# Moving the reload of gated outputs and the tail's loads in the last head of a recurrent mixer

## The chip, the cores and the metric

The kernel runs on one core of one Trainium2 chip. The metric is device time in microseconds (us) of one execution. The engines are TensorE (PE; PEld is its weight load), VectorE (DVE), ScalarE (ACT), GpSimd (POOL) and SyncE (SP). Each executes its own queue of instructions in order; SP, ACT and POOL also issue DMA transfers, each on a queue of its own, and all transfers run on the core's 16 DMA engines.

## The reference, cut to what matters

One step of a two-layer trunk over 640 tokens (512 latent, 128 context) of width 1024. Layer 0 is a gated grouped-query attention. Layer 1, in which the change lies, is a bidirectional gated linear recurrence (HGRN2) with 8 heads of 128 keys and 128 values:

```python
proj = h @ w_in                      # q, f_fw, f_bw, i_in, g: five blocks of 1024 columns
qh = silu(heads(q)); vh = heads(i_in)
forget = lb + (1 - lb) * sigmoid(f)  # for each direction
k = (1 - lb) * sigmoid(-f)
S = exp(b_last) * S + einsum(k * exp(b_last - b), v)     # scan, forward and backward
o = scores @ v + (q * exp(b)) @ S
o = rms_norm(o_fw + flip(o_bw), norm_gain)
gated = (o * silu(g)).astype(h.dtype)
out = gated @ w_out
x = layer_norm(ALPHA * x + gate * out, ln_gain, ln_bias)
```

Outputs are the new latent and context tokens, the attention's keys and values of the context, and the final states of the recurrence (`new_s`).

## The kernel before

All matrix products are done in a split form: an operand is written as a rounded high part and the remaining low part (`hi`, `lo`), and three products (hi·hi, hi·lo, lo·hi) are accumulated. A cast on ACT makes the high part, a subtraction on DVE or POOL the low part.

**Layer 1 runs head by head.** For each of the 8 heads `proj_gen` makes the five projections of the head on TensorE, and `gla_gen` then makes its recurrence. The two are generators that stop at `yield`; the main loop runs the projections of head h and, through a `Lane` with estimated times, lets the recurrence of head h − 1 advance between them. The projections of the last head (h = 7) have 23 steps: two for each of five token tiles (n = 0 to 9, the products `vgps`, lines 1377 and 1381), four for the query (n = 10 to 13, `rps`, lines 1403 to 1405), four for each direction's forget gate (n = 14 to 21), and one that ends them. The weights come as 512 KB pieces into three raw buffers (`raw`, line 239, on SP's queue); a cast on ACT (line 260) and a subtraction on DVE (line 262) turn a piece into `hi` and `lo`, and free its buffer. `pump` asks for raw pieces up to two ahead of their use: all 40 pieces of `rec_w_in`, then the 8 of `rec_w_out`.

**The recurrence** (`gla_gen`) is a tree over levels 0 to 6 of token blocks. At each level a key copy on ACT (`kc`, line 1651), in some levels also a query copy (`At`, line 1656), prepares TensorE's score products (`lv`, lines 1677 and 1683), and two DVE multiplications (`A`, lines 1701 and 1706) apply the decay. The blocks near the diagonal are gathered in `near` (lines 1668 and 1728) and written into the score tile `At` by four copies on POOL (`spread`, line 1715); the far blocks go there by copies on ACT (`place`, line 1721). Then come key transposes (`kp`, line 1766) and their copy `kt` (line 1768), state products (`sp`, line 1772), the state update on DVE (`S`), the final states' copies `ns` (line 1782) and stores (`new_s`, line 1783), the output products (`op`), the root of the mean square on POOL (`rstdo`, line 211), and the transposed, gated output (`oT`, line 1809). Heads 0 to 6 take their levels in pairs; the last head takes them one by one, with `spread` in level 4. The tile `ns` shares its buffer (tag `kc`) with the key copies.

**The gated outputs** of the first heads have no room in SBUF, since heads 1 to 6 use seven block products instead of eight and keep sums of the tokens (`thi`, `tlo`) in the buffers `hhi` and `hlo`. Those outputs are stored to DRAM (`gd`). With the last head the sums are done with, and `reload_gen` takes the two buffers as `ghi` and `glo`, loads the stored outputs into `glo` (line 1624, SP's queue, five loads of 320 KB), and makes for each a cast on ACT (line 1627) and a subtraction on DVE (line 1628). The three heads that end later write into `ghi` and `glo` directly (lines 1819 and 1820).

**The tail.** After the last projections the main program runs the end of head 6's recurrence, and then head 7's recurrence interleaved with the first output products (`outp`, lines 1211 to 1213) and the last pieces of `rec_w_out` (`tail_steps`). The epilogue of the output (class `Out`) multiplies with the gate (`y`, line 1257), adds the residual (line 1260) and normalises. It needs the gate rows (`gate[1]`, two loads of 512 KB, line 339) and the residual tiles `x1` (512 KB each, line 1913), all on POOL's queue. In the kernel before, the gate and the first two residual tiles are asked for before head 6's recurrence is finished.

**Order.** This half of the program is not run in the order in which it is written. A planner places each instruction on its engine's queue, by a model of time: of those that are ready, the one written first goes first, so a later-written instruction that is ready sooner overtakes. `tc.keep_in_program_order` ties an instruction behind all that was written before it on its engine, and `tc.issue_after(ins)` ties what is written in its block behind `ins` on that engine; neither adds a wait.

Of the kernel before, what the change touches and what calls it, by code (L numbers as in the profile page):

```python
# [11 lines left out]
F32 = mybir.dt.float32  # L12
# [6 lines left out]
P = 128  # L19
D = 1024  # L20
# [3 lines left out]
NT = TT * P  # L24
# [4 lines left out]
RH = 8  # L29
# [20 lines left out]
RES_AT = 6  # L50
SEVEN = range(1, RH - 1)
FORMS_AT = 3
D_GLA = 5.5
D_LEV = 2.7
D_PAIR = 6.0
# [12 lines left out]
def view(t, off, dims):  # L68
    base = t[:]
    return bass.AP(base.tensor, base.offset + off, [list(base.ap[0])] + [list(d) for d in dims])  # L70
# [76 lines left out]
def drain(gen):  # L147
    for _ in gen:
        pass
# [3 lines left out]
def hybrid_step(ctx: ExitStack, tc: tile.TileContext, a: dict, o: dict):  # L153
    nc = tc.nc
    PSUM = bass.MemoryType.PSUM

    def pool(name, bufs, **kw):
        return tc.tile_pool(name=name, bufs=bufs, **kw)
# [178 lines left out]
    def gate_load(layer, eng):  # L337
        for s in range(2):
            eng.dma_start(gate[layer][:, s, :], gated[layer][s:s + 1, :].to_broadcast((P, D)))
# [96 lines left out]
    gate = [None, None]  # L436
# [3 lines left out]
    def lpool(name, bufs):  # L440
        return left.enter_context(pool(name, bufs))
# [661 lines left out]
    side = Side()  # L1103
# [220 lines left out]
    KF, KB, QB, QF = 0, NT, 2 * NT, 3 * NT  # L1324
# [3 lines left out]

    last_gate = []
    outs_done = []  # L1330
    vg_done = []

    def held():
        st = ExitStack()
# [265 lines left out]
    def token_forms():  # L1600
        f11, f12, f22, f21 = sums
        for f, i, j in ((f11, 0, 0), (f12, 0, 1), (f22, 1, 1), (f21, 1, 0)):
            hi, lo = (t[:, 4 * i:4 * i + 4, slice(*HALVES[j])].bitcast(F32) for t in (h1hi, h1lo))
            with tc.issue_after(vg_done[0]):
                nc.vector.tensor_tensor(f, hi, lo, ALU.add)
            yield
        for dst, x, y in ((f11, f12, f11), (f12, f22, f12), (f22, f11, f22)):
            nc.vector.tensor_tensor(dst, x, y, ALU.subtract)
            yield
        nc.vector.tensor_tensor(f21, f21, f22, ALU.add)  # L1610
        yield
        for (hi, lo), f in zip(tokens, (f11, f22, f12, f21)):
            nc.scalar.copy(hi, f)
            yield
            nc.vector.tensor_tensor(lo, f, hi.bitcast(F32), ALU.subtract)
            yield

    def reload_gen():
        ghi = hp.tile([P, KT, NT], F32R, tag="hhi", name="ghi")
        glo = hp.tile([P, KT, NT], F32R, tag="hlo", name="glo")  # L1620
        gated_out.extend((ghi, glo))
        todo = list(spilled)
        for k in todo:
            nc.sync.dma_start(glo[:, k, :].bitcast(F32), gd[k])
        for k in todo:
            yield
            nc.scalar.copy(ghi[:, k, :], glo[:, k, :].bitcast(F32))
            nc.vector.tensor_tensor(glo[:, k, :], glo[:, k, :].bitcast(F32), ghi[:, k, :].bitcast(F32), ALU.subtract)

    cs = ExitStack()  # L1630
    g2 = cs.enter_context(pool("g2", 2, side="right"))
# [8 lines left out]
    def gla_gen(h, H):  # L1640
        A, T, v, g = H["A"], H["T"], H["vg"][:, :, 0, :], H["vg"][:, :, 1, :]
# [6 lines left out]
        def kcopy(w, tag="kc"):  # L1648
            nb = NT // (2 * w)
            kc = g1.tile([P, NT], F32, tag=tag, name="kc")  # L1650
            nc.scalar.copy(view(kc, 0, [[2 * w, nb], [w, 2], [1, w]]), view(A, KF, [[2 * w, nb], [KB - KF + w, 2], [1, w]]))  # L1651
            return kc

        def qcopy(w):
            nb = NT // (2 * w)
            nc.scalar.copy(view(At, 0, [[2 * w, nb], [w, 2], [1, w]]), view(A, QB, [[2 * w, nb], [QF - QB + w, 2], [1, w]]))
            return At

        kc = kcopy(1)
        yield D_GLA  # L1660
        near = g1.tile([P, 32 * TT], F32, tag="near", name="near")
        At = g1.tile([P, NT], F32, tag="At", name="At")

        def blocks(t, w):
            return t.rearrange("p (a b) -> p a b", b=w)
# [46 lines left out]
        def spread():  # L1712
            for b in range(4):
                r = slice(32 * b, 32 * b + 32)
                nc.gpsimd.tensor_copy(blocks(At[r, :], P)[:, :, r], blocks(near[r, :], 32))  # L1715

        def place(lev, pt):
            w = 1 << lev
# [11 lines left out]
        if pairs:  # L1730
            for lev in (1, 3, 5):
                if lev == 1:
                    yield D_TAIL
                    lane.finish(1)
                k2, _, _ = decay(lev, "on" if lev < 5 else None)
                yield D_FIRST if lev == 1 else D_PAIR if h < RH - 2 else 2 * D_LEV
                pt = wide(bank2("lv"))
                late = scores(pt[:, 512:], lev + 1, k2, None)
                with tc.issue_after(late):
                    scores(pt, lev, k1, q1)  # L1740
                k1, q1, last = decay(lev + 1, "kc" if lev < 5 else None, lev < 5)
                if lev < 5:
                    merge(lev, pt)
                    merge(lev + 1, pt[:, 512:])
                else:
                    spread()
                    place(5, pt)
                    place(6, pt[:, 512:])
        else:
            for lev in range(1, 7):  # L1750
                yield D_LEV
                pt = wide(bank2("lv"))
                scores(pt, lev, k1, None)
                k1, _, last = decay(lev, "kc" if lev < 4 else None)
                if lev < 5:
                    merge(lev, pt)
                else:
                    place(lev, pt)
                if lev == 4:
                    spread()  # L1760
# [56 lines left out]
        ghi, glo = gated_out  # L1817
# [51 lines left out]
    def wo_piece(n, after=()):  # L1869
        nh, i = OUT1[n]  # L1870
        hi, lo = slots[2 * n], slots[2 * n + 1]
        wo[nh, i] = tuple(t.rearrange("p (k n) -> p k n", k=2) for t in (hi, lo))
        split_piece(hi, lo, ("rec_w_out", nh, i), nc.vector, after)

    def wr_slots():
        w = wr.tile([P, 2, 1024], F32R, tag="w", name="rw")
        slots.extend(w[:, i, :] for i in range(2))
# [9 lines left out]
    side = token_forms()  # L1887
    for h in range(RH):
        H = {} if h else H
        if h == RH - 1:  # L1890
            sxs.close()
            side = reload_gen()
            next(side, None)
        for n, dt in enumerate(proj_gen(h, H, False) if h else first):
            lane.advance(dt)
            if h or n >= FORMS_AT:
                next(side, None)
            if h == 0 and n == RES_AT:
                residual.compute()
                residual.loads()  # L1900
        lane.add(gla_gen(h, H))
# [4 lines left out]
    ghi, glo = gated_out  # L1906
# [4 lines left out]
    def load_resid(tt, t):  # L1911
        resid[tt] = t
        tc.keep_in_program_order(nc.gpsimd.dma_start(t, x1a[tt]))

    def out_k(tt, k):
        if tt not in outs:
            outs[tt] = bank2("outp", "pj" if tt < 2 else "b2")
        for nh in range(2):
            out_mms(outs[tt], tt, nh, ghi, glo, [k])

    def tail_steps():
        wr_slots()
        wo_piece(3)
        for tt in range(2):
            out_k(tt, 1)
        yield
        w2 = gsp.tile([P, 5, 1024], F32R, tag="gs", name="w2")
        w3 = h1p.tile([P, 5, 1024], F32R, tag="h1lo", name="w3")
        slots.extend(t[:, i, :] for t in (w2, w3) for i in range(5))
        wo_piece(4)  # L1930
        out_k(0, 2)
        yield
        todo = [(tt, k) for k in range(2, KT - 1) for tt in range(2)][1:]
        for n in range(5):
            if n < 3:
                wo_piece(n + 5)
            for tt, k in todo[2 * n:2 * n + 2]:
                out_k(tt, k)
            yield
        for ks in ((0,), (1,), (2,), (3, 4, 5), (6,)):  # L1940
            for k in ks:
                out_k(2, k)
            yield

    while not lane.gens[0][2]:
        lane.step(lane.gens[0])
    gate[1] = g2.tile([P, 2, D], F32, tag="A", name="gate1")
    gate_load(1, nc.gpsimd)
    xp = lpool("xp", 1)
    load_resid(0, xp.tile([P, D], F32, name="x1"))  # L1950
    load_resid(1, g2.tile([P, 2 * NT], F32, tag="T", name="x1")[:, :D])
    for tt in range(2):
        out_k(tt, 0)
    lane.finish(1)
    steps = tail_steps()
    for _ in lane.gens[0][0]:
        next(steps, None)
    drain(steps)
    gx.close()
# [129 lines left out]
```

## Time and profile before

| | us |
|---|---|
| median of 3 runs | 825.15 |
| the three runs | 823.31, 829.16, 825.15 |
| the profiled execution | 824.67 |
| its span | 822.9 |
| mean granted TensorE clock | 0.994 |

The time of an execution is that of the whole program on the device; the span is the profile's, from its first to its last instruction. In a timeline a row gives the start in us from the span's start, the length in us, the engine, the line of the kernel, the operation, output and inputs, and their shapes; where the engine was idle before, the length of that pause and the instruction that ended it stand in brackets. `x5` merges five neighbours. SPq, ACTq and POOL's rows of DMA give the time of issue, not that of the transfer. Rows of issues give the KB of each transfer and the median us from its issue to its landing.

### The profile page before, as it was taken

Reading aid. Unit: us, or ns where it says so; the run is one execution under the profiler, and the core shown is the slowest. Engines: PE = TensorE matmul, PEld = TensorE weight load, DVE = VectorE, ACT = ScalarE, POOL = GpSimd, SP = SyncE. Lnnn points to the kernel's source line nnn. Section 1 sums busy time; section 2 is a strip of 40 time slices with the busy share of each in tenths; the row PEclk is TensorE's granted clock in tenths of the full one; section 3 lists DMA queues with packets and bytes.
Section 4 is the critical chain, followed back from the end, with each engine's and each line's share of the span. In section 5 each row is a group of like instructions: output and inputs, shape, how many; then the busy total and the mean of one; then the engine's idle time right before and its main releaser. Section 6 shows DMA issues by size and latency. Waiting matters only on the chain.

```text
span 822.9 us, 19277 instructions
## 1 busy us (share of the span) xinstructions
PE 793.2 (96%) x7953; PEld 701.2 (85%) x7953; DVE 597.8 (73%) x1083; ACT 447.8 (54%) x890; POOL 214.9 (26%) x261
## 2 busy tenths in 40 slices
PE   8999999999999989999999999999999999998994
PEld 6779999878888766888999999999989999896874
DVE  3667767686678885676898787778687866977376
ACT  2252545566566786132565766667474847754242
POOL 0124001353434943011500324122321304131021
PEclk9999999999999999999999999999999999999998
DMA  9944243334130150621432343324132425224041
GB/s 324 395 147 165 103 154 131 103 106 153 52 129 27 40 191 30 227 103 54 136 104 66 91 114 98 105 68 126 54 126 65 114 90 171 84 89 172 31 156 76
DMA packets 36630, 98.12 MB, mean 119 GB/s; under 512 B 5296, under 2 KB 12480, under 8 KB 36544
## 3 DMA queue, kind: packets, MB, share of 16 engines
q1 hardware_dynamic: 25872, 78.95, 28.7%
q0 software_dynamic: 4768, 14.18, 6.0%
q10 hardware_dynamic: 5904, 3.78, 1.5%
q8 instruction: 62, 1.02, 0.5%
q14 instruction: 24, 0.20, 0.1%
HBM read 86.06 MB, written 10.83 MB: 118 GB/s over the span
## 4 chain that ended last, share of the span: by engine, by line
PE 78%; DVE 8%; ACT 5%; DMA 4%; issue 2%; POOL 2%; SPq 0%; ACTq 0%; DVEq 0%; POOLq 0%
PE vgps L1381 7%; PE vgps L1377 4%; PE pot L948 4%; PE outp L1211 4%; PE rps L1449 3%; PE rps L1403 3%; PE outp L1213 3%; PE outp L1212 3%; PE rps L1405 3%; PE rps L1404 3%; PE pt L1034 3%; PE rps L1451 3%; PE rps L1450 3%; PE acc L566 3%; PE lv L1677 2%
## 5 line engine op out<-in xcount | busy, mean ns | idle before, releaser
L1027 POOL TENSOR_SCALAR p<-p,rc 128x640 f32<-128x640 f32 x64 | 57.1, 897 | 115.2 <-DVE rc L1026 98.0
L1715 POOL COPY At<-near 32x160 f32<-32x160 f32 x32 | 14.2, 443 | 195.9 <-PE lv L1683 176.0
L1021 ACT ACTIVATE p<-sc,nm 128x640 f32<-128x640 f32 x64 | 51.2, 802 | 25.3 <-DVE nm L1016 15.6
L1016 DVE TENSOR_REDUCE nm<-sc 128x1 f32<-128x640 f32 x64 | 51.7, 816 | 12.6 <-PE sc L922 12.5
L1403 PE MATMUL rps<-h1hi,rw 128*128 128x320 f32 x176 | 55.4, 315 | 0.0
L1404 PE MATMUL rps<-h1lo,rw 128*128 128x320 f32 x176 | 54.4, 309 | 0.0
L1405 PE MATMUL rps<-h1hi,rw 128*128 128x320 f32 x176 | 54.4, 309 | 0.0
L1034 PE MATMUL pt<-small,p 128*128 128x128 f32 x320 | 49.0, 277 | 3.0 <-DVE pts L926 1.2
L1381 PE MATMUL vgps<-rw,h1hi 128*128 128x512 f32 x180 | 48.4, 393 | 0.1
L1034 PEld LDWEIGHTS pt<-small,p 128*128 128x128 f32 x320 | 36.5, 140 | 12.0 <-issue 5.6
L1651 ACT COPY kc<-A 128x640 f32<-128x640 f32 x47 | 37.5, 798 | 13.5 <-DVE A L1701 7.5
L926 ACT COPY pts<-pt 128x512 f32<-128x512 f32 x64 | 36.1, 590 | 14.7 <-PE pt L1034 14.5
L921 PE MATMUL sc<-kk,X 128*128 128x320 f32 x128 | 42.4, 340 | 1.7 <-ACT p L1021 1.6
L1721 ACT COPY At<-lv 32x160 f32<-32x160 f32 (+1 forms) x48 | 15.9, 331 | 51.0 <-PE lv L1683 50.6
L948 PE MATMUL pot<-pts,vv 128*64 128x256 f32 x320 | 38.3, 384 | 2.1 <-DVE pts L926 2.0
L378 PE MATMUL gps<-hhi,whi 128*128 128x320 f32 x128 | 40.0, 312 | 0.1
L379 PE MATMUL gps<-hlo,whi 128*128 128x320 f32 x128 | 39.6, 309 | 0.0
L380 PE MATMUL gps<-hhi,wlo 128*128 128x320 f32 x128 | 39.5, 309 | 0.0
L1381 PEld LDWEIGHTS vgps<-rw,h1hi 128*128 128x128 f32 x180 | 33.0, 188 | 7.1 <-DVE vg L1397 0.5
L922 PE MATMUL sc<-klo,X 128*128 128x320 f32 x128 | 38.5, 310 | 0.0
L1381 PE MATMUL vgps<-wspare,h1hi 128*128 128x512 f32 x140 | 38.2, 394 | 0.0
L387 PE MATMUL qmm<-whi,hhi 128*128 128x256 f32 x120 | 35.0, 292 | 0.1
(347 smaller groups left out, 2624.5 us busy)
## 6 DMA issues: line engine op xcount, KB each, us to landing
raw<-in_rec_w_in SPq DMA_DIRECT2D x40, 512.0 KB, 3.8
raw<-in_ada_m SPq DMA_DIRECT2D x16, 512.0 KB, 8.3
raw<-in_attn_w_in SPq DMA_DIRECT2D x16, 512.0 KB, 4.6
raw<-in_ada_s SPq DMA_DIRECT2D x16, 512.0 KB, 3.7
adaraw<-in_ada_c SPq DMA_DIRECT2D x11, 512.0 KB, 5.4
raw<-in_attn_w_out SPq DMA_DIRECT2D x8, 512.0 KB, 3.9
raw<-in_rec_w_out SPq DMA_DIRECT2D x8, 512.0 KB, 4.5
raw<-in_ada_c SPq DMA_DIRECT2D x5, 512.0 KB, 4.4
```

The lines of the kernel that those rows point to most:

```text
L378: nc.tensor.matmul(ps[:, :320], w.hi(k)[:, c], hhi[:, k, t], start=(k == 0), stop=False)
L379: nc.tensor.matmul(ps[:, :320], w.hi(k)[:, c], hlo[:, k, t], start=False, stop=False)
L921: nc.tensor.matmul(out, X[:, h, t0:t0 + P], kk[:, c, k0:k1], start=True, stop=False)
L948: nc.tensor.matmul(pot[j * HD:(j + 1) * HD, :CW], vv[:, slot, c * HD:(c + 1) * HD], moving[j], start=first, stop=last)
L1016: nc.vector.tensor_reduce(nm[:, 0:1], sc[:, :, :320], AX.XY, ALU.max, negate=True)
L1021: return nc.scalar.activation(halves(p[:]), sc[:, :, :320], AF.Exp, bias=nm[:, 0:1], accum_out=su[:, 0:1])
L1027: nc.gpsimd.tensor_scalar(p, p, rs[:, 0:1], 1.0, ALU.mult, ALU.mult)
L1034: nc.tensor.transpose(pt[:, i * 256 + q * P:i * 256 + (q + 1) * P], ps[q][:, (k0 + i) * P:(k0 + i + 1) * P], ident)
L1381: nc.tensor.matmul(out, h1hi[:, k, t], wvg[i][:, k % 4].rearrange("p e n -> p (e n)"), start=(k == 0), stop=(k == KT - 1))
L1403: nc.tensor.matmul(ps[:, j, :320], hi[:, k, :], h1hi[:, k, t], start=(k == 0), stop=False)
L1404: nc.tensor.matmul(ps[:, j, :320], hi[:, k, :], h1lo[:, k, t], start=False, stop=False)
L1405: nc.tensor.matmul(ps[:, j, :320], lo[:, k, :], h1hi[:, k, t], start=False, stop=(k == KT - 1))
```

## The change

Two things are moved; no computation is added or left out.

1. `reload_gen` takes its two buffers when the last head starts, as before, but stops there. It goes on at step 6 of the last head's projections, where it writes the five loads, rests during steps 7 to 11, and writes one pair of cast and subtraction per step from step 12 on. Each cast is tied behind the key copy that was written last at that time. Before, the loads were written at the head's start, and the pairs at steps 0 to 4, with no tie.
2. The loads of the gate and of the first two residual tiles are no longer written before the end of head 6, but inside head 7's recurrence, after the step that writes `spread`, and tied behind the last of its four copies on POOL.

```diff
+RELOAD_AT = 6
+RELOAD_OFF = ((), range(7, 12))
...
         todo = list(spilled)
+        yield
         for k in todo:
             nc.sync.dma_start(glo[:, k, :].bitcast(F32), gd[k])
         for k in todo:
             yield
-            nc.scalar.copy(ghi[:, k, :], glo[:, k, :].bitcast(F32))
+            with tc.issue_after(last_kc[0]):
+                nc.scalar.copy(ghi[:, k, :], glo[:, k, :].bitcast(F32))
             nc.vector.tensor_tensor(glo[:, k, :], ...)
...
-            nc.scalar.copy(view(kc, ...), view(A, KF, ...))
+            last_kc[:] = [nc.scalar.copy(view(kc, ...), view(A, KF, ...)).ins]
...
-                nc.gpsimd.tensor_copy(blocks(At[r, :], P)[:, :, r], blocks(near[r, :], 32))
+                spread_done[:] = [nc.gpsimd.tensor_copy(blocks(At[r, :], P)[:, :, r], blocks(near[r, :], 32)).ins]
...
-            next(side, None)
+            next(side)
         for n, dt in enumerate(proj_gen(h, H, False) if h else first):
             lane.advance(dt)
-            if h or n >= FORMS_AT:
+            if n >= (FORMS_AT if h == 0 else RELOAD_AT if h == RH - 1 else 0) and n not in RELOAD_OFF[h == RH - 1]:
                 next(side, None)
...
+    def tail_loads():
+        with tc.issue_after(spread_done[0]):
+            gate[1] = g2.tile([P, 2, D], F32, tag="A", name="gate1")
+            gate_load(1, nc.gpsimd)
+            xp = lpool("xp", 1)
+            load_resid(0, xp.tile([P, D], F32, name="x1"))
+            load_resid(1, g2.tile([P, 2 * NT], F32, tag="T", name="x1")[:, :D])
...
     while not lane.gens[0][2]:
         lane.step(lane.gens[0])
-    gate[1] = g2.tile([P, 2, D], F32, tag="A", name="gate1")
-    gate_load(1, nc.gpsimd)
-    xp = lpool("xp", 1)
-    load_resid(0, xp.tile([P, D], F32, name="x1"))
-    load_resid(1, g2.tile([P, 2 * NT], F32, tag="T", name="x1")[:, :D])
...
     steps = tail_steps()
+    spread_done.clear()
     for _ in lane.gens[0][0]:
+        if spread_done:
+            tail_loads()
+            spread_done.clear()
         next(steps, None)
```

More of the change, by code (lines that the diff above doesn't have):

```diff
@@ L1330, in hybrid_step @@
     outs_done = []
-    vg_done = []
+    vg_done, spread_done, last_kc = [], [], []
     def held():
@@ L1650, in kcopy @@
             kc = g1.tile([P, NT], F32, tag=tag, name="kc")
-            nc.scalar.copy(view(kc, 0, [[2 * w, nb], [w, 2], [1, w]]), view(A, KF, [[2 * w, nb], [KB - KF + w, 2], [1, w]]))
+            last_kc[:] = [nc.scalar.copy(view(kc, 0, [[2 * w, nb], [w, 2], [1, w]]),
+                                         view(A, KF, [[2 * w, nb], [KB - KF + w, 2], [1, w]])).ins]
             return kc
```

## The prediction

> **What bounds the kernel now.** I read the page first.
>
> ```profile
> span 822.9 us, 19277 instructions
> ...
> PE 793.2 (96%) x7953; PEld 701.2 (85%) x7953; DVE 597.8 (73%) x1083; ACT 447.8 (54%) x890; POOL 214.9 (26%) x261
> ```
>
> TensorE is busy for 793.2 of 822.9 us. The change removes no matrix work, so all that it can win is TensorE's idle time, and only that part of the 29.7 us that lies where it moves something: from the start of the last head (about 687 us) to the end of that head's scores (about 765 us). The profiled execution took 824.67 us, 1.8 over its span; the median of the three runs shown is 825.15, 0.5 above it. I make the sum on the profiled execution and add that 0.5.
>
> Next I read busy time by stretches of time and, for what ended each idle piece, the timelines of single engines.
>
> ```profile
> 745.00:750.00 5.00, 4.15 (x133) 3.33 (x131) 4.41 (x8) 3.21 (x5) 0.00 (x0) 1.00 0.99 382
> 750.00:755.00 5.00, 3.17 (x90) 2.15 (x88) 3.07 (x6) 1.67 (x2) 0.00 (x0) 1.00 0.21 82
> 763.00:775.00 12.00, 11.83 (x118) 9.65 (x117) 4.82 (x13) 3.00 (x7) 1.26 (x4) 1.00 0.00 1
> ```
>
> The columns are stretch, length, busy PE, PEld, DVE, ACT, POOL, granted clock, DMA share, GB/s. From 745 to 755 TensorE is idle for 0.85 + 1.83 = 2.68 us; in its first half the DMA engines are full (0.99, 382 GB/s). From 763 to 775 they carry nothing. The clock is 1.00, so it plays no part.
>
> ```profile
> 698.19 0.63 PE L1677 MATMUL lv<-A,kc 128*32 128x32 f32 x40 [0.88 <-ACT kc L1651]
> ...
> 708.53 0.52 PE L1677 MATMUL lv<-A,kc 128*32 128x32 f32 x38 [0.78 <-DVE A L1706]
> ```
>
> These are the two other TensorE gaps in reach, in the reload's stretch: 0.88 us for a key copy on ACT, 0.78 us for a decay step on DVE. So 0.88 + 0.78 + 2.68 = 4.34 us, 0.5% of the run, is the most that the change can win.
>
> **Part 1, the reload of gated outputs.** It has five loads on SP's queue and five pairs of an ACT cast and a DVE subtraction.
>
> ```profile
> 662.46 24.49 SPq L239 DMA_DIRECT2D raw<-in_rec_w_in  x4
> 687.32 2.22 SPq L1624 DMA_DIRECT2D glo<-gd  x5
> 690.70 55.68 SPq L239 DMA_DIRECT2D raw<-in_rec_w_out  x8
> ```
>
> *The loads.* The program writes the reload before the last head's projections, so also before the last three of these rec_w_in loads, which the projections' weight steps call for; yet it stands behind all four in the queue. The order is the planner's, by when a load's buffer is free: glo takes the buffer of the token sums, in use until head 6's last products. Written six steps later, the loads still come before the first rec_w_out load, which is written at step 14. I therefore expect them at the same place in the queue, at about 687 us: cost nothing, gain nothing. Were they really later, this would win:
>
> ```profile
> out_new_s<-ns ACTq DMA_DIRECT2D x16, 64.0 KB, 1.8
> ...
> out_new_s<-ns ACTq DMA_DIRECT2D x2, 64.0 KB, 7.2
> ...
> 697.13 1.00 ACT L1651 COPY kc<-A 128x640 f32<-128x640 f32 x1 [2.91 <-DMA out_new_s<-ns]
> ```
>
> The state stores land in 1.8 us at the median of sixteen, but in 7.2 us beside the reload (the second row is from 684 to 700 us). Their source shares its buffer with the key copy, so ACT waits 2.91 us and TensorE the 0.88 above. With the reload gone from there the 0.88 goes; with it in place it stays. I take 0 and keep 0.88 for a rival.
>
> *The casts move for certain*, since each is tied behind the key copy written last when its step comes.
>
> ```profile
> L1627 ACT CAST ghi<-glo x5: 711/732/748, 692.9 to 705.2; 128x640 fp32r<-128x640 f32 x5
> L1628 DVE TENSOR_TENSOR glo<-glo,ghi x5: 817/819/828, 693.8 to 706.0; 128x640 fp32r<-128x640 f32 x5
> ...
> 703.19 0.83 DVE L1628 TENSOR_TENSOR glo<-glo,ghi 128x640 fp32r<-128x640 f32 x1 [0.62 <-ACT ghi L1627]
> 703.93 0.69 DVE L1397 TENSOR_TENSOR vg<-vgps,low 128x512 f32<-128x512 f32 x1
> ...
> 707.57 0.82 DVE L1706 TENSOR_TENSOR A<-A,Tb 128x640 f32<-128x640 f32 x1
> ```
>
> Five casts of 0.73 us (3.7 us of ACT) and five subtractions of 0.82 us (4.1 us of DVE) leave 693 to 707 us. Two of them stand in the chain to the 0.78 gap. The subtraction at 703.19 makes DVE wait 0.62 for its cast and ends 0.74 later, where the next row starts; the one at 706.0 takes 0.8 more ahead of the decay step at 707.57, on which TensorE waits. Taking 0.8 to 1.5 us out of a chain that is 0.78 late removes that gap: gain 0.8. Next late there is TensorE's own queue, which is full.
>
> *Where they go* must hold them:
>
> ```profile
> 712.82 0.73 ACT L1651 COPY kc<-A 128x640 f32<-128x640 f32 x1 [0.23 <-DVE A L1701]
> 714.68 1.05 ACT L260 CAST w<-raw 128x1024 fp32r<-128x1024 f32 x1 [1.13 <-DMA raw<-in_rec_w_out]
> ...
> 719.42 0.73 ACT L1651 COPY kc<-A 128x640 f32<-128x640 f32 x1
> ...
> 724.37 2.04 ACT L1721 COPY At<-lv 32x160 f32<-32x160 f32 x6 [3.59 <-PE lv L1683]
> ...
> 723.78 0.83 DVE L1701 TENSOR_TENSOR A<-A,T 128x640 f32<-128x640 f32 x1 [0.82 <-PE lv L1683]
> ...
> 727.17 1.18 DVE L1512 TENSOR_SCALAR T<-s,omlb,lbt 128x640 f32<-128x640 f32 x1 [1.72 <-ACT s L1501]
> ...
> 727.77 1.04 PE L1766 MATMUL kp<-small,A 128*128 128x128 f32 x8
> ```
>
> At step 12 the last key copy written is the one at 712.82, from step 13 on the one at 719.42. The first cast (0.73) fits ACT's 1.13 us wait before 714.68; the other four, 2.9 us, fit the 3.59 us wait before 724.37. On DVE the last four subtractions, at 0.74 each back to back, are 3.0 us against idle pieces of 0.82 and 1.72 us. If all came before the decay at 723.78, its pair would end 3.0 − 0.82 = 2.2 us later, at about 727.6 instead of 725.4 (727.17 less the wait of 1.72), just ahead of the transposes at 727.77 that read it. Bounds: 0, and 1 us should a wait slip past them. I take 0.2, near the first, since the subtractions have no reader before the output products:
>
> ```profile
> L1211 PE MATMUL outp<-wx,ghi x10: 389/389/499, 738.9 to 800.7; 128*128 128x512 f32 x10
> ```
>
> **Part 2, the tail's loads.** Four loads of 512 KB on POOL's queue (two gate rows, two residual tiles) leave the stretch where the last weights come in.
>
> ```profile
> 739.26 1.12 POOL L339 DMA_DIRECT2D gate<-gated  x2 [9.03 <-PE op L1789]
> ...
> gate<-gated POOLq DMA_DIRECT2D x2, 512.0 KB, 5.4
> raw<-in_rec_w_out SPq DMA_DIRECT2D x2, 512.0 KB, 6.8
> x<-x1a POOLq DMA_DIRECT2D x2, 512.0 KB, 7.8
> ...
> raw<-in_rec_w_out SPq DMA_DIRECT2D x8, 512.0 KB, 4.5
> ...
> 747.50 1.06 ACT L260 CAST w<-raw 128x1024 fp32r<-128x1024 f32 x1 [1.22 <-DMA raw<-in_rec_w_out]
> ...
> 752.78 1.04 ACT L260 CAST w<-raw 128x1024 fp32r<-128x1024 f32 x1 [3.35 <-DMA raw<-in_rec_w_out]
> ...
> 749.29 0.39 PE L1212 MATMUL outp<-rw,ghi 128*128 128x512 f32 x1 [0.85 <-issue]
> ...
> 754.50 0.56 PE L1677 MATMUL lv<-A,kc 128*32 128x32 f32 x40 [1.82 <-ACT kc L1651]
> ```
>
> Beside them two weight loads take 6.8 us where the median of all eight is 4.5. ACT waits in order for the second, 3.35 us, with the key copy queued behind the weight's cast; TensorE waits 1.82 us for that copy. Landing in 4.5 us instead of 6.8 it is there 2.3 us sooner, and the scores at 754.50 could start at 752.2. TensorE reaches them at 754.50 − 1.82 = 752.68 from its own queue. So the 1.82 goes. The other 0.85 us is a gap that the profile lays to no engine, in the stretch where DMA is full. If it is a slow fetch of instructions, it goes too, and the scores start at 752.2: gain 2.3. From below the gain is 0, if the load is slow for another reason. I take 2.0.
>
> [...] No run here shows what that gap is.
>
> *The price.* The loads start behind the spread, with the last products' epilogue as their first reader:
>
> ```profile
> 763.21 1.39 POOL L1715 COPY At<-near 32x160 f32<-32x160 f32 x4 [18.91 <-DVE near L1668]
> ...
> 786.66 1.29 DVE L1257 TENSOR_TENSOR y<-outp,gate 128x512 f32<-128x512 f32 x2
> ```
>
> Issued from 764.6 (763.21 + 1.39), at 1.12 us of POOL for two, the last is out by 766.8 and lands by 774.6 even in 7.8 us, 12 us before 786.66, in a stretch with no other transfers. POOL itself is free there: the spread waited 18.91 us for its input. Queued behind the loads is only the last head's square root, whose input comes from TensorE's last product of that head. Cost 0; without that cover it would be the lateness itself, beyond 12 us.
>
> **Sum:** −0.8 + 0.2 − 2.0 = −2.6; 824.67 − 2.6 = 822.1 for a profiled execution, about 822.5 as a median (825.15 − 2.6).
>
> **Rivals.** *The reload really starts later* (for: it is written later, and SP waits long for raw buffers; against: the planner's order above). Then the 0.88 goes as well: 825.15 − 3.5 = 821.7. Chance 0.2.
>
> *No gain.* The planner puts the four casts not into ACT's 3.59 us but behind the copies at 724.37. ACT's queue is then unbroken up to the copy that feeds the state products:
>
> ```profile
> 730.22 1.03 ACT L1768 COPY kt<-kp 128x1024 f32<-128x1024 f32 x1
> ...
> 731.30 2.05 PE L1772 MATMUL sp<-vg,kt 128*128 128x128 f32 x16
> ```
>
> TensorE takes those products 0.05 us after the copy, so 2.9 us of casts ahead of it are 2.9 us of TensorE, against gains of 2.8: about 825.2. Chance 0.14.
>
> *Slower.* The five reload loads fall behind the rec_w_out load that waits for a raw buffer:
>
> ```profile
> 717.13 29.25 SPq L239 DMA_DIRECT2D raw<-in_rec_w_out  x6
> ```
>
> Issued after it, from 717.5 to 719.7, the first would land 4 to 8 us later, at 721.5 to 725.5. The first cast, ready on ACT at 713.55, would hold everything behind it for 8 to 12 us, the weight cast, the sigmoids and the key copy of 719.42 among it. From the cast's end at 722.2 or later, that work, at most 719.42 + 0.73 − 714.68 = 5.5 us, would have to run before the scores that DVE waited for until 723.78: 4 to 8 us late for TensorE. I take 5, since its waits inside would shrink; less the gains of 2.8 that is 825.15 + 2.2 = 827.4. It decides if the reload stands behind that load, not if it is only behind the first rec_w_out at 690.70. For it: writing at step 6 makes the loads younger. Against: they are ready earlier. Chance 0.12.
>
> **Chances.** Forecast 0.5 (822.5, its own range 820.8 to 824.5), later reload 0.2, no gain 0.14, slower 0.12; 0.04 for an order of the planner that I do not foresee. The lowest end is all of the 4.34: 820.8; the three runs before reach from 823.31 to 829.16, so I add 1.3 below and set the high end at 826.5, which leaves out the slower case. About 1% is what a measurement of this kernel tells from no change: faster means under 816.9, slower over 833.4. No case reaches either; for the unforeseen and the runs' own scatter I leave 0.03 and 0.04.
>
> **What would show it.** In the changed profile: the reload's loads still at 687 to 690 us (or later, with the state stores back at 1.8 us); the casts at about 713 and 721 to 724; no wait of TensorE at 708 for a decay; gate and residual loads from about 762; the last two weight loads near 4.5 us and no wait of 1.82 us before the scores. I am wrong if ACT waits for glo, if TensorE waits near 731 for the key transposes' copy, or if the weight loads stay at 6.8 us.

## The result, and the profile after

| | before | after |
|---|---|---|
| median, us | 825.96 (11 runs, 822.86 to 829.83) | 821.64 (11 runs, 818.26 to 822.77) |
| ratio to before, 95% interval | | 0.9938 (0.9917 to 0.996) |
| profiled execution, us | 824.67 | 820.92 |
| its span, us | 822.9 | 819.2 |

The change makes the kernel 4.3 us shorter by the medians, 3.75 us by the two profiled executions. The forecast was 822.5, 2.65 us less. The interval leaves the kernel faster, by 0.4 to 0.8%, and within 1%. A second measurement of the changed kernel gave 820.08 against 825.68, ratio 0.9932 (0.9913 to 0.9951).

The page of the changed kernel, span and busy time:

```profile
span 819.2 us, 19274 instructions
...
PE 792.4 (97%) x7953; PEld 700.9 (86%) x7953; DVE 598.3 (73%) x1083; ACT 447.0 (55%) x890; POOL 215.1 (26%) x261
```

TensorE's work is what it was, to 0.8 us (793.2 before). Of the 3.7 us between the two spans, 2.9 are idle time of TensorE that is gone. Its busy time by stretches, changed kernel, columns as in the prediction:

```profile
745.00:750.00 5.00, 5.00 (x133) 3.99 (x121) 5.00 (x10) 3.79 (x6) 0.00 (x0) 1.00 0.35 108
750.00:755.00 5.00, 5.00 (x97) 3.73 (x96) 5.00 (x12) 1.10 (x3) 0.00 (x0) 1.00 0.00 2
763.00:775.00 12.00, 11.84 (x93) 10.37 (x92) 3.68 (x10) 2.29 (x5) 0.00 (x0) 1.00 0.47 164
775.00:787.00 12.00, 11.54 (x54) 9.12 (x54) 6.00 (x11) 5.36 (x21) 2.84 (x4) 1.00 0.63 215
```

From 745 to 755 TensorE is busy all the time, where it was idle for 2.68 us. The DMA share there fell from 0.99 and 0.21 to 0.35 and 0, and rose from 0 to 0.47 at 763 to 775. Timelines of the engines, changed kernel (lines are shifted by 2 to 5 against before):

```profile
687.10 2.23 SPq L1627 DMA_DIRECT2D glo<-gd  x5
697.40 1.00 ACT L1655 COPY kc<-A 128x640 f32<-128x640 f32 x1 [4.66 <-DMA out_new_s<-ns]
698.46 0.62 PE L1682 MATMUL lv<-A,kc 128*32 128x32 f32 x40 [1.36 <-ACT kc L1655]
...
707.59 0.53 PE L1682 MATMUL lv<-A,kc 128*32 128x32 f32 x38
712.35 0.73 ACT L1631 CAST ghi<-glo 128x640 fp32r<-128x640 f32 x1
718.65 2.61 ACT L1631 CAST ghi<-glo 128x640 fp32r<-128x640 f32 x4
723.52 2.03 ACT L1726 COPY At<-lv 32x160 f32<-32x160 f32 x6 [2.26 <-PE lv L1688]
748.57 1.06 ACT L262 CAST w<-raw 128x1024 fp32r<-128x1024 f32 x1 [0.28 <-DMA raw<-in_rec_w_out]
759.49 1.38 POOL L1720 COPY At<-near 32x160 f32<-32x160 f32 x4 [17.11 <-DVE near L1673]
760.82 1.07 POOL L341 DMA_DIRECT2D gate<-gated  x2
761.87 1.06 POOL L1918 DMA_DIRECT2D x<-x1a  x2
782.95 1.29 DVE L1259 TENSOR_TENSOR y<-outp,gate 128x512 f32<-128x512 f32 x2
```

- The reload's loads stand at 687 us, as before.
- The copy that waits for the state's store, and TensorE behind it at 698, wait on.
- At 707.59 TensorE no longer waits for a decay step.
- The casts are where the prediction put them, and ACT still waits 2.26 us for TensorE behind them, so they hold nothing.
- ACT's wait for the last piece of `rec_w_out` is 0.28 us instead of 3.35, and the wait of 1.82 us at the scores is gone.
- The tail's loads start at 760.8.

Their landing times in the changed kernel, stretch 740 to 770 us (KB each, median us from issue to landing):

```profile
gate<-gated POOLq DMA_DIRECT2D x2, 512.0 KB, 4.7
x<-x1a POOLq DMA_DIRECT2D x2, 512.0 KB, 7.3
raw<-in_rec_w_out SPq DMA_DIRECT2D x2, 512.0 KB, 3.4
```

The weights land in 3.4 us instead of 6.8. The last residual tile, issued by 762.93 (761.87 + 1.06), is there at about 770.2 (762.93 + 7.3), 12 us before the epilogue begins to read these loads at 782.95.

### The profile page after: what moved, and what is told of

Its sections match the earlier page's. It is cut to its first block, busy times and chain, and to the rows that moved or that the text cites. A ratio compares the mean times of both kernels' runs of the same rounds, so it can differ in the third digit from the quotient of the medians.

```text
span 819.2 us, 19274 instructions
## 1 busy us (share of the span) xinstructions
PE 792.4 (97%) x7953; PEld 700.9 (86%) x7953; DVE 598.3 (73%) x1083; ACT 447.0 (55%) x890; POOL 215.1 (26%) x261
## 3 DMA queue, kind: packets, MB, share of 16 engines
q8 instruction: 62, 1.02, 0.5%
## 4 chain that ended last, share of the span: by engine, by line
PE 80%; DVE 8%; DMA 4%; ACT 3%; issue 2%; POOL 2%; SPq 0%; DVEq 0%; ACTq 0%; POOLq 0%
PE vgps L1383 8%; PE vgps L1379 4%; PE outp L1213 4%; PE outp L1215 4%; PE outp L1214 4%; PE rps L1451 4%; PE pot L950 3%; PE rps L1405 3%; PE rps L1407 3%; PE rps L1406 3%; PE pt L1036 3%; PE rps L1453 3%; PE rps L1452 3%; PE acc L568 3%; PE lv L1682 2%
```

## The experiments

Times are medians in us; ratios are to the kernel before, measured beside each, with their 95% intervals. "Idle" is TensorE's in the profiled execution, for four stretches: 684 to 712 (state store, decay), 712 to 745 (the casts' new place), 745 to 755 (last weights; with the reload alone its last gap ends at 755.18, in the next stretch), 755 to 787.

| kernel | time | ratio | 684–712 | 712–745 | 745–755 | 755–787 |
|---|---|---|---|---|---|---|
| before | 825.96 | 1 | 1.75 | 0.15 | 2.68 | 0.62 |
| after | 821.64 | 0.9938 (0.9917 to 0.996) | 1.37 | 0.08 | 0 | 0.62 |
| reload alone | 825.91 | 0.9991 (0.997 to 1.0012) | 1.50 | 0.08 | 2.28 | 0.71 |
| tail loads alone | 824.19 | 0.9966 (0.9943 to 0.9988) | 1.80 | 0.15 | 0 | 0.62 |
| casts not tied | 822.57 | 0.9939 (0.9914 to 0.9963) | 2.49 | 0.13 | 0 | 0.61 |
| reload on POOL's queue | 820.66 | 0.9933 (0.9911 to 0.9955) | 0 | 0.53 | 0 | 0.62 |
| own buffer for the store | 820.71 | 0.9921 (0.989 to 0.9951) | 0 | 0.08 | 0 | 0.62 |
| residual tiles early | 821.22 | 0.9927 (0.99 to 0.9954) | 1.22 | 0.08 | 1.10 | 0.61 |
| reload behind weights | 821.66 | 0.992 (0.9887 to 0.9953) | 0 | 2.24 | 0 | 0.62 |
| casts behind far blocks | 822.44 | 0.9936 (0.9916 to 0.9956) | 2.35 | 0.72 | 0.56 | 0.61 |

An interval is 3.3 to 5.5 us wide. The times settle the large steps; for steps of 1 us the profile has to do.

**Each part alone.** The first kernel is the changed one with the tail's loads back at their old place; the second is the changed one with the old reload.

```diff
-    def tail_loads(): ...            # and its call
+    gate[1] = ...; gate_load(1, nc.gpsimd); load_resid(0, ...); load_resid(1, ...)   # ahead of out_k(tt, 0)
```

> Part 1 alone: the reload as changed, the gate and residual loads at their old place. Queues of PE, DVE, ACT and SP as in the changed kernel, POOL's as before. If the two parts add up, this is worth the smaller share: about 0.8 to 1.2 us under the kernel before (TensorE's wait of 0.78 us for a decay gone; the wait for the key copy at 698 us stays at 0.9 to 1.4), with the 0.85 us gap and the 1.82 us wait at 749 and 754 us still there. Rival: the casts' move only helps because the weight loads came sooner; then this is no faster than before.

```diff
-        yield
...
-            with tc.issue_after(last_kc[0]):
...
-            if n >= (FORMS_AT if h == 0 else RELOAD_AT if h == RH - 1 else 0) and n not in RELOAD_OFF[h == RH - 1]:
+            if h or n >= FORMS_AT:
```

> Part 2 alone: the gate and residual loads behind the spread, the reload as before. If the slow weight loads come from those four loads, the last two weight loads land in 3.4 to 4.5 us, the wait of 1.82 us goes, and so does the gap of 0.85 us if it belongs to the full DMA engines: 2.7 us under the kernel before, or 1.8 if the gap stays. The wait of 0.78 us for a decay stays. Rival: the weight loads are slow from something else, or the gain needs part 1; then under 1 us.

The reload alone is not told from the kernel before (0.9991); the tail's loads alone make it faster (0.9966, the interval below 1). TensorE's timeline and the landing times from 735 to 760, reload alone:

```profile
750.07 0.50 PE L1215 MATMUL outp<-rw,glo 128*128 128x512 f32 x1 [0.62 <-issue]
755.18 0.56 PE L1682 MATMUL lv<-A,kc 128*32 128x32 f32 x40 [1.84 <-ACT kc L1655]
```

```profile
raw<-in_rec_w_out SPq DMA_DIRECT2D x2, 512.0 KB, 6.7
```

and the timeline with the tail's loads alone:

```profile
699.29 0.63 PE L1680 MATMUL lv<-A,kc 128*32 128x32 f32 x40 [0.92 <-ACT kc L1653]
709.62 0.52 PE L1680 MATMUL lv<-A,kc 128*32 128x32 f32 x38 [0.78 <-DVE A L1709]
```

The two parts are apart, as the sum had it. With the reload alone both gaps of the last weights stay and the 0.78 us wait for the decay step is gone; with the tail's loads alone it is the other way round. The gap of 0.62 to 0.85 us laid to "issue" goes with the tail's loads.

**What holds the last weights.** Gate rows late, the two residual tiles (1 MB) at their old place:

```diff
     def tail_loads(): ...
-            load_resid(0, ...); load_resid(1, ...)
+    load_resid(0, ...); load_resid(1, ...)       # ahead of out_k(tt, 0)
```

> The changed kernel with the two residual loads (1 MB) back at their old place and only the two gate loads (1 MB) behind the spread; all other queues as in the changed kernel. If the weight loads are slowed by the bytes that share the DMA engines with them, half of the bytes cost about half: the last weight load lands in 4.5 to 5.5 us instead of 3.4 (6.7 with all four), TensorE's wait before the scores is 0 to 1 us instead of 1.8, and the time is 0.5 to 1.5 us over the changed kernel. Rival: the residual loads, issued last and closest to the last weight load, carry the whole loss, 2 us or more. The gap of 0.85 us that the profile lays to nothing is there if a stretch of full DMA engines brings it.

Timelines of ACT and TensorE, and the landing times from 735 to 760, of both weight loads and then of each (738 to 744, 744.2 to 750), residual tiles early:

```profile
751.81 1.05 ACT L262 CAST w<-raw 128x1024 fp32r<-128x1024 f32 x1 [1.80 <-DMA raw<-in_rec_w_out]
753.54 0.56 PE L1682 MATMUL lv<-A,kc 128*32 128x32 f32 x40 [1.10 <-ACT kc L1655]
```

```profile
raw<-in_rec_w_out SPq DMA_DIRECT2D x2, 512.0 KB, 4.0
```

```profile
raw<-in_rec_w_out SPq DMA_DIRECT2D x1, 512.0 KB, 3.2
raw<-in_rec_w_out SPq DMA_DIRECT2D x1, 512.0 KB, 4.9
```

Half of the bytes leave a wait of 1.10 us, and no "issue" gap, at a DMA share of 0.92 from 745 to 750. The median of 4.0 us hides that the two loads differ: ACT waits for the last one, which takes 4.9. That last load takes 6.6 us with all four loads beside it (reload alone), 4.9 with two and 3.4 with none (changed kernel), and TensorE's idle time goes with it: 2.46 (0.62 + 1.84), 1.10 and 0 us. So the waits come from the bytes beside the weights.

**Whether the reload's place matters.** The loads on POOL's queue in program order, which really puts them six steps later (702.5 us), and the state's copies in a buffer of their own, which lets the key copy go without the store:

```diff
-            nc.sync.dma_start(glo[:, k, :].bitcast(F32), gd[k])
+            tc.keep_in_program_order(nc.gpsimd.dma_start(glo[:, k, :].bitcast(F32), gd[k]))
```

> The changed kernel with the five reload loads on POOL's queue, kept in program order there, so that they really start after the first steps of the last head (about 704 us); all other queues as in the changed kernel but for SP, which loses them. If the reload's traffic is what holds the state stores, these land in about 2 us, ACT's wait of 4.66 us before the key copy and TensorE's of 1.36 us go: 1.2 to 1.4 us under the changed kernel. Rival: the stores are slow beside the weight load alone; then the time stays. Against a gain: a cast at 712 us could wait for its load.

```diff
-        ns = g1.tile([P, 2, P], F32, tag="kc", name="ns")
+        ns = g1.tile([P, 2, P], F32, tag="ns", name="ns")
```

> The changed kernel with a buffer of its own for the state copies, so that the key copy needs no longer wait for the state stores; the order on every queue is that of the changed kernel. The stores stay slow (about 7 us), but ACT's wait of 4.66 us and TensorE's of 1.36 us go: 1.0 to 1.4 us under the changed kernel. Rival: behind the key copy the next thing is just as late (the load of the state, or the square sums on ACT), and less than 0.5 us is won.

Busy time from 684 to 712 and the store's landing from 684 to 700, reload on POOL's queue; then the landing with the own buffer:

```profile
684.00:712.00 28.00, 28.00 (x370) 25.80 (x369) 21.40 (x36) 20.19 (x42) 10.55 (x15) 1.00 0.50 168
```

```profile
out_new_s<-ns ACTq DMA_DIRECT2D x2, 64.0 KB, 2.9
```

```profile
out_new_s<-ns ACTq DMA_DIRECT2D x2, 64.0 KB, 7.5
```

Either way TensorE has no gap from 684 to 712: without the reload beside it the store is short (2.9 us), and with the own buffer nobody waits for it (7.5 us, and no wait). That shows the prediction's chain for the 0.88 us: reload, store, shared buffer, key copy, TensorE. The later reload gives 0.53 us back, at a wait of TensorE for a weight's subtraction.

The own buffer has the lowest idle time, so it was measured directly against the changed kernel, on one chip:

> The changed kernel once more, beside its version with an own buffer for the state stage (second run of this call), on one chip. Both theories: about 0.994 of the time before; its profile keeps the wait of TensorE near 698 us behind the key copy that waits for the state's store (1.4 us).

> The changed kernel with the state's store in a buffer of its own, directly against the changed kernel (first run of this call). If the 1.4 us that TensorE no longer waits near 698 us is worth its length at the end: 0.9983 of the changed kernel's time, 1.4 us less. If it is given back later: the same time. The times of this kernel scatter by 2 to 4 us, so 1.4 us may stay within the scatter.

The changed kernel took 820.08 (819.22 to 821.29, 6 runs), the own buffer 820.71 (816.98 to 824.29, 8 runs; 0.9941, 0.9916 to 0.9967). TensorE's wait at 698 was 0.73 us in this profile of the changed kernel, and none with the own buffer. What is left of the store's wait is too small for these times, and no version was found that beats the changed kernel by more than they tell.

**What the tie does.** The casts without `issue_after`:

```diff
-            with tc.issue_after(last_kc[0]):
-                nc.scalar.copy(ghi[:, k, :], glo[:, k, :].bitcast(F32))
+            nc.scalar.copy(ghi[:, k, :], glo[:, k, :].bitcast(F32))
```

> The changed kernel without the tie of the casts to the key copies; the reload is still written at step 6 and its casts from step 12. By the planner's order the five casts go back to 692 to 706 us, now behind the recurrence's work where both are ready; the loads stay at 687 us. If the tie is what moves the work, the casts and subtractions are in that stretch again and TensorE's wait at 708 us returns in part (0 to 0.8 us): 0 to 0.8 us over the changed kernel. Rival: the later place in the program is enough, the chain to the scores is as free as with the tie, and the time is that of the changed kernel.

The planner puts the casts back to 692.6 to 706.7 us, though they are written from step 12 on. The timeline of TensorE, casts not tied:

```profile
707.29 0.73 ACT L1654 COPY kc<-A 128x640 f32<-128x640 f32 x1
708.07 0.53 PE L1681 MATMUL lv<-A,kc 128*32 128x32 f32 x38 [0.27 <-ACT kc L1654]
710.00 0.42 PE L1405 MATMUL rps<-h1hi,rw 128*128 128x320 f32 x1 [1.01 <-DVE vg L1399]
```

It waits 0.27 and 1.01 us near 708 to 710 instead of 0.78. So it is the tie and not the step of writing that moves the casts; the time (0.9939) does not tell the two apart.

**The two rivals with a price.** The reload's loads tied behind the third load of `rec_w_out`, which waits for a raw buffer; and the casts tied behind the copies of the far blocks:

```diff
-RELOAD_AT = 6
-RELOAD_OFF = ((), range(7, 12))
+RELOAD_AT = 18
+RELOAD_OFF = ((), ())
...
-                (pass_on if src[0][:3] == "rec" else pin)(nc.sync.dma_start(raw, piece(src)))
+                raw_dma[src] = (pass_on if src[0][:3] == "rec" else pin)(nc.sync.dma_start(raw, piece(src))).ins
...
-        for k in todo:
-            nc.sync.dma_start(glo[:, k, :].bitcast(F32), gd[k])
+        with tc.issue_after(raw_dma[("rec_w_out",) + OUT1[2]]):
+            for k in todo:
+                nc.sync.dma_start(glo[:, k, :].bitcast(F32), gd[k])
```

> The slower rival of the prediction, built: the five reload loads stand on SP's queue behind the third rec_w_out load, which waits for a raw buffer until 716 us, and the five casts on ACT between the key copy of 717 us and the far-block copies of 723 us. The first load lands at about 721 us, the last up to 4 us later; ACT waits for it with the far-block copies, the sigmoids and the copy of the key transposes behind. By the price in the prediction that is 5 us, less 1.4 us since the state stores are free of the reload: about 3 to 4 us over the changed kernel. Rival: ACT has enough room before the key transposes' copy at 729 us, and the loss is under 1 us.

```diff
-RELOAD_OFF = ((), range(7, 12))
+RELOAD_OFF = ((), range(7, 16))
...
-                nc.scalar.copy(blocks(At[r, :], P)[:, :, o_], blocks(pt[r, :w * TT], w))     # in place()
+                last_kc[:] = [nc.scalar.copy(...).ins]
```

> The no-gain rival of the prediction, built in part: the casts are tied behind the far-block copies of head 6. By the planner two of them stand ahead of the copy of the key transposes, three behind it; the order of a few products on TensorE shifts with them. If ACT's queue is unbroken from 723 us to that copy, as the profile has it, two casts there are 1.3 us of delay for the state products and 0.5 to 1.5 us of TensorE over the changed kernel. Rival: TensorE has projections to run meanwhile, and the time stays.

The timeline of the first, ACT and TensorE:

```profile
719.01 0.73 ACT L1634 CAST ghi<-glo 128x640 fp32r<-128x640 f32 x1 [0.53 <-DMA glo<-gd]
722.27 3.19 ACT L1634 CAST ghi<-glo 128x640 fp32r<-128x640 f32 x4 [2.53 <-DMA glo<-gd]
732.27 3.68 PE L1780 MATMUL sp<-vg,kt 128*128 128x128 f32 x16 [2.24 <-ACT kt L1776]
```

ACT does wait for `glo`, 0.53 and 2.53 us, and TensorE at the state products for 2.24. The products then take 3.68 us where they took 2.05: the clock was halved behind the gap (below). So this mechanism costs 2.24 + 1.63 = 3.9 us in this execution, and the way it is built here gives 1.4 us back at the store. In the second kernel three of the casts stand behind the copy `kt` and two ahead of it; the gap at the state products is 0.62 us. What causes another gap, of 0.56 us at 750, is not known. Both stay faster than before.

**The clock behind the gap.** With the reload alone the profile shows something that the first profile of before does not: a halved clock right behind the gap at 753. Two more profiles of the kernel before ask if it has that too:

> The kernel before, unchanged, for a second profile of it. In the profile of the reload moved alone, the two gaps at 749 and 753 us (0.62 and 1.84) were followed by 3.3 us at half the granted clock (756.5 to 759.8), worth 1.7 us; in the first profile of before the same gaps (0.85 and 1.82) were not. Theory: the loss hangs on where the gaps fall in the clock's own windows, so some executions of before have it too: then this profile shows a granted clock of about 0.5 for 3 us between 755 and 760, and 1.7 us more from there to the end. Rival: the clock holds in before; then it is 1.00 there again, as in the first.

> A third profile of the kernel before, for the same question. Theory: in some of the three profiles the granted clock is halved for about 3 us behind the gap at 753 us, at a price of 1.7 us. Rival: in none. Two profiles without it would not exclude it, one with it shows it.

Busy time from 755 to 760 in the first profile of before (the clock is the third number from the right), and the next scores behind the gap in its timeline:

```profile
755.00:760.00 5.00, 5.00 (x66) 3.93 (x60) 5.00 (x11) 1.46 (x2) 0.00 (x0) 1.00 0.02 5
```

```profile
757.95 0.56 PE L1677 MATMUL lv<-A,kc 128*32 128x32 f32 x40
```

The same stretch, and TensorE's timeline, in the second profile of before:

```profile
755.00:760.00 5.00, 5.00 (x79) 3.76 (x71) 3.90 (x8) 0.72 (x1) 0.00 (x0) 0.66 0.01 2
```

```profile
749.54 0.40 PE L1212 MATMUL outp<-rw,ghi 128*128 128x512 f32 x1 [0.68 <-issue]
...
754.80 0.63 PE L1677 MATMUL lv<-A,kc 128*32 128x32 f32 x40 [1.87 <-ACT kc L1651]
...
756.81 0.63 PE L1211 MATMUL outp<-rw,ghi 128*128 128x512 f32 x1
...
758.98 0.40 PE L1211 MATMUL outp<-w,ghi 128*128 128x512 f32 x1
...
759.77 0.56 PE L1677 MATMUL lv<-A,kc 128*32 128x32 f32 x40
```

A product of 512 columns that takes 0.40 us takes 0.63 from 756 to about 758.5. From the scores behind the gap to the next ones it is 4.97 us here (754.80 to 759.77) and 3.45 in the first profile (754.50, quoted in the prediction, to 757.95): the halved clock costs 1.5 us more. In the profile of the reload alone the same stretch is 5.03 us (755.18 to 760.21), and the clock from 755 to 760 is 0.66 too. The third profile of before has gaps just as large (0.76 and 1.94 us) and a clock of 1.00. So two of the four profiles that have these gaps (three of before, one of the reload alone) have the loss as well, and the size of the gap does not decide it. In the ten profiles without them the clock from 755 to 760 is 1.00.

## Why the prediction was right, and where it was not

**The ceiling, TensorE's idle time in reach.** Right as to where: the idle time that was won lies at 708 and 745 to 755. The step that failed is "The clock is 1.00, so it plays no part". That held for the one profile it was read from. In the second of three profiles of the same kernel the clock is halved behind the gap at 753, which costs 1.5 us more, so the most that could be won was 4.34 + 1.5 there.

**The reload's loads, 0.** Right: 687.32 became 687.10. TensorE's wait for the store's copy was 0.88 us before and 1.36 after in the two profiles compared, which looks like a loss of 0.48. It is within the scatter: three profiles of before have 0.88, 1.61 and 0.98; four with the same casts and nothing changed at the store (after twice, reload alone, residual tiles early) have 1.36, 0.73, 1.45 and 1.21. The means are 1.16 and 1.19. The highest wait, 2.34 us, is that of the casts behind far blocks, with a store that lands in 8.4 us instead of 7.0 to 7.7; a small loss from moving the casts is not ruled out.

**The casts' move, −0.8 and +0.2.** The first is right: the gap of 0.78 us at 708.53 is gone in the kernels whose casts moved, and stands at 0.78 to 0.80 in the profiles with the old reload (the casts not tied wait 0.27 and 1.01 us there, as said). The crowding was 0, not 0.2: TensorE's idle time from 712 to 745 went from 0.15 to 0.08 us. The cover held as named: the last of the casts ends before 721.3 and ACT's next work waits for TensorE until 723.52. By the time alone this part cannot be told from nothing (0.9991, 0.997 to 1.0012), which also holds the 0.6 us of the prediction.

**The tail's loads, −2.0.** The mechanism was right and the size too small: 2.68 us. Both parts of the gap went, the 1.82 us behind the last weights and the 0.85 us laid to "issue". The prediction took a landing of 4.5 us, the median of all eight weight loads, and that median holds loads which also had company (in the changed kernel the eight have 3.6). What counts is the last load alone. It took 6.7 us before and takes 3.4 in the changed kernel, that of a stretch without other loads. By the prediction's own arithmetic a landing of 4.5 us would have won 2.3 us at most. With the residual tiles early, at 4.9 us and without the "issue" gap, 1.10 us stay, so at 4.5 some 0.7 us would have stayed (an estimate).

As to the second gap, the prediction left open what it is. It went. It is in all four profiles with four tail loads beside the weights (0.85, 0.68, 0.76, 0.62 us) and in none of the ten others, so it comes with that traffic. The traces fit a late fetch. The page of the profile lists a queue "instruction" (q8, 62 transfers, 1.02 MB, so 16 KB each). One of them runs from 746.77 to 747.76 in the first profile of before, and the gap from 748.44 to 749.29. So it ends 0.7 us before the gap and 1.5 us before TensorE goes on. In the changed kernel the same transfer ends at 744.74, 2.7 us before TensorE starts the same product (747.45). That is argued and not shown, since no run moves this transfer alone.

**The price of later loads, 0.** Right: TensorE's idle time from 755 to 787 is 0.62 in both kernels.

**The sum.** With the sizes measured it is −0.78 − 2.68 = −3.5 us against −2.6 forecast; the profiled executions differ by 3.75. That they come so near is in part chance: between these two the wait at 698 grew by 0.48, and 0.8 us are busy time, which no term of the sum has. The medians differ by 4.3, and by 5.6 in the second measurement. The halved clock fits the rest: 1.5 us in two profiles of four is 0.75 us in the mean, and 3.5 + 0.75 = 4.2, which lies in both intervals (3.3 to 6.9 us, and 4.0 to 7.2). That share comes from four profiles, one of them of the reload alone, and is an estimate. The forecast time is nearer (822.5 against 821.64) than the forecast gain (2.65 against 4.3), since the three runs that it started from have a median 0.8 us below that of all eleven: that is luck.

**The rivals.** *The reload really starts later* did not happen, though its 821.7 is the time nearest to the measured one: that is chance. Made on purpose it takes TensorE's wait at 698 away, as said, and returns 0.53 us elsewhere. *No gain* did not happen, and its price of 2.9 us for four casts was tested only in part: the planner put two casts behind the far blocks ahead of the copy that feeds the state products, 1.35 us of ACT, and the products waited 0.62 us. *Slower* did not happen either. Its place was right (ACT waits for `glo`, TensorE at 732). Its price of 5 us came out at 3.9, by two terms, one of which it did not have: 2.24 us of waiting and 1.63 us of halved clock behind it. It did not have the credit either: with the reload gone from 687, the wait for the store goes, so that kernel is not slower than before (0.992).

## What to carry to other kernels

When the last weights arrive late, look at what else is on the DMA engines in that stretch and at the first reader of each: four loads of 512 KB, which still had 12 us to spare when they were issued 21 us later, took 2.7 us from TensorE. Size a wait by the one load that is waited for, and its gain by a landing without company, not by a median over all. Gaps of 1.84 to 2.24 us cost 1.5 to 1.6 us more here through the clock, in some executions and not in others, so read more than one profile before the clock is ruled out.

## What the runs showed of the hardware

**Behind some gaps of 1.8 to 2.2 us TensorE's clock was halved for 3.4 us.** It was so behind gaps of 1.84, 1.87 and 2.24 us (reload alone, second profile of before, reload behind weights), at 1.5 to 1.6 us each, and was not behind gaps of 1.82, 1.94 and 2.34. Busy time in the second profile of before, cut where the clock changes:

```profile
751.68:755.09 3.41, 1.54 (x40) 0.99 (x39) 1.45 (x4) 1.67 (x2) 0.00 (x0) 1.00 0.02 6
755.09:758.50 3.41, 3.41 (x37) 2.69 (x24) 3.41 (x7) 0.72 (x1) 0.00 (x0) 0.50 0.01 2
```

The other two halved stretches are 3.41 us long as well (756.53 to 759.94 and 732.41 to 735.82), and in all three the whole gap lies in the 3.41 us ahead. In the first profile of before the clock changes at 10.75, 14.16 and 816.29 us, 1 and 235 steps of 3.413 us apart; in the changed kernel at 9.34, 12.75 and 811.47, 1 and 234 steps apart. So where a trace shows a change, its steps can be counted from there. The most idle time in one of them near the gap is 1.83 us in the first profile of before (751.44 to 754.85) and 1.72 with the casts behind far blocks, whose gap of 2.34 is split between two. So the place of the gap among the steps fits these five gaps. It is no limit to rely on: 1.83 and 1.84 us lie on its two sides, and at 9.34 us in the changed kernel the clock was halved after a step with 1.17 us of idle time (5.93 to 9.34).

The same halving comes and goes between 290 and 300 us, far ahead of the change, in executions of either kernel. Busy time there, the changed kernel's second profile:

```profile
292.00:298.00 6.00, 5.60 (x23) 4.71 (x23) 5.83 (x16) 3.58 (x8) 2.27 (x3) 0.50 0.86 302
```

and its first:

```profile
292.00:298.00 6.00, 4.82 (x31) 3.56 (x31) 6.00 (x16) 3.80 (x8) 2.06 (x3) 1.00 0.87 309
```

There it costs little: the second profile reaches the scores at 698.47 us after 0.73 us of waiting, the first at 698.46 after 1.36, so the second was at most about 0.6 us later until then. TensorE has idle time in that stretch, which the slower products fill (0.40 us of 6 against 1.18), and DVE is the full engine (5.83 and 6.00 us).

**A small store was as slow as the loads beside it.** The 64 KB stores of the state land in 7.0 to 8.4 us beside the reload (5.4 to 7.4) and a weight load (7.2 to 8.2), in 2.9 to 3.6 when the reload is elsewhere, and in 1.8 at the median of all before. The key copy that shares the buffer of their source waited for them for 2.91 us in the first profile of before and for 4.66 in the changed kernel, and not at all with a buffer of its own.
